# Additions of the staged block sums on VectorE, held in program order

## The chip, the cores and the metric

The kernel runs on one core of one Trainium2 chip. The metric is the device time of one execution in microseconds (us), median of several runs. The core's engines work side by side: PE (TensorE, matrix products), DVE (VectorE), ACT (ScalarE), POOL (GpSimd, here mostly an issuer of transfers) and SP (SyncE, the issuer of the weight transfers). Each engine runs its own instructions strictly in the order in which they stand in its program, and waits where an operand isn't there yet.

## The reference, cut to what matters

One block of a network on 256 tokens of width 2048, all in float32:

```python
h = rms_norm(x, norm_mix_pre)
proj = einsum('bsd,dn->bsn', h, w_in)          # 2048 x 14336 weights, split in 11 parts
y_a = cb * causal_dwconv3(cc * cv, conv_mix_w)
y_b = hgrn2(...)                               # chunked linear recurrence, 8 heads
y_m = softmax(qh @ kh.T / 16) @ vh             # attention over 256 memory rows, 4 heads
merged = (sigmoid(ga) * (y_a @ w_branch[0]) + sigmoid(gb) * (y_b @ w_branch[1])
          + sigmoid(gm) * (y_m @ w_branch[2]))
x = x + rms_norm(merged @ w_out, norm_mix_post)
up_g, up_v = split(rms_norm(x, norm_ffn_pre) @ w_ffn_up)
act = gelu(causal_dwconv3(up_g, conv_ffn_w) + conv_ffn_b) * up_v
x = x + rms_norm(act @ w_ffn_down, norm_ffn_post)
```

The weights are far larger than the on-chip memory and are read once, in the order in which the products need them.

## The kernel before, in words

**Units.** The weight stream is cut into pieces of 1 MB (tile `w`, three buffers) and every piece into two units of 1024 columns. For each unit ACT rounds the weights to `wh` (`halve`, L1107) and DVE forms the remainder `wl = w - wh` (L1108); PE then multiplies by both (L1165 and L1166 where the weights stand still in the array, eight pairs a unit; L1176 to L1178 where the operand does). `wh` and `wl` have four buffers each. The main loop traces `load_to(n + 2)`, `multiply(n)`, `load_to(n + 3)`, then one step of the background queue (norm of x, attention `attend` L298, the recurrence), then one step of the staging. So the `wl` of unit n + 3 is traced ahead of what the staging traces in turn n.

**Stages of the program.** Units 0 to 15 are the lead (memory keys, tile `a_mem`), 16 to 35 the rest of the memory keys and values; 36 to 51 attention queries, with the four attention heads in the background; 52 to 99 three parts of the recurrence's input; 100 to 115 its values; then gates, branches and convolution up to unit 307; `w_out` 308 to 339; then the feed-forward part, whose down projection comes last.

**Staging.** The down projection uses sums of weight blocks for 26 groups (p, j). These sums are made ahead of time in a scratch in DRAM: `load_` (L820) brings 1 MB of `wdown` into a tile `stage` (two buffers) by a DMA that POOL issues (L826), `add_` (L828) makes three additions on DVE in place (one of 1024 columns, L831; two of 512, L834), `store_` (L836) writes the tile to `sums` by another DMA of POOL (L839). A group takes six turns of the main loop: the first traces the store of the group before, the fifth L831, the sixth both L834 and the load of the next group. These turns are units 36 to 115 (thirteen groups) and 250 to 329 (thirteen more), by `STAGE` (L34). The down projection reads the sums back much later.

**Order.** What is traced is not yet the order on an engine: a scheduler lays out each engine's instructions from the dependencies, its own idea of how long things take, and what is ready first. `pin` (L82, `tc.keep_in_program_order`) is an exception: the instruction given to it must stand behind the instruction of its engine that was traced ahead of it. The kernel uses it in the middle and last stages, not in the staging. The scheduler has put the additions of all 26 groups on DVE into the first fifth of the program; those of the second span of turns stand far ahead of the turns that trace them.

Of the kernel before, what the change touches and what calls it, by code (L numbers as in the profile page):

```python
# [13 lines left out]
ALU = mybir.AluOpType  # L14
# [50 lines left out]
def block_kernel(ctx: ExitStack, tc: tile.TileContext, xT, lead, cols, wkvT, wkvN, winT, winN, wbr, wout, wup, wlead, wdown, grow, xN, masks, out):  # L65
    nc = tc.nc
# [15 lines left out]
    pin = tc.keep_in_program_order  # L82
# [734 lines left out]
    def stage(groups):  # L817
        tiles = {}

        def load_(n):  # L820
            if n < len(groups):
                p, j = groups[n]
                tiles[n] = ph.tile([P, 2048], F32, name="stage", tag="stage", bufs=2)
                if n < 2:
                    nc.vector.memset(tiles[n][:, 0:1], 0.0)
                nc.gpsimd.dma_start(tiles[n], wdown[p * DP + j])  # L826

        def add_(n, part):  # L828
            t = tiles[n]
            if part == 0:  # L830
                nc.vector.tensor_tensor(t[:, 0:1024], t[:, 0:1024], t[:, 512:1536], op=ALU.add)  # L831
                return
            for c, low in ((1024, 0), (1536, 1024)):
                nc.vector.tensor_tensor(t[:, c:c + 512], t[:, c:c + 512], t[:, low:low + 512], op=ALU.add)  # L834

        def store_(n):  # L836
            p, j = groups[n]
            stored[p, j] = dram.tile([P, 2048], F32, name=f"sums{p}_{j}")
            nc.gpsimd.dma_start(stored[p, j], tiles.pop(n))  # L839

        load_(0)
        yield
        for n in range(len(groups)):
            for step in range(1, 7):
                if step == 1 and n:
                    store_(n - 1)
                if step == 5:
                    add_(n, 0)
                if step == 6:
                    add_(n, 1)  # L850
                    load_(n + 1)
                yield
        store_(len(groups) - 1)
        yield
# [427 lines left out]
```

## Time and profile before

| | |
|---|---|
| median of 3 runs | 1823.41 us (1821.53 to 1827.84) |
| the profiled execution: time, span | 1823.14 us, 1821.4 us |
| PE busy | 1757.0 us (96%) |
| DVE busy | 1344.9 us (74%) |
| ACT busy | 964.3 us (53%) |
| POOL busy | 36.7 us (2%) |
| moved by DMA | 406.63 MB, 223 GB/s over the span |

The busy share is an average over the whole span. Views that cut the span into stretches (busy time, granted clock and DMA by stretch), the waits by engine and the order of time on one engine say where it is lower. PE's granted clock has two levels, 1.2 and 2.4 GHz, and is given as a share of the higher one. Times of PE are partly modelled, since products overlap in the array, and a few per cent of its records can be missing.

### The profile page before, as it was taken

Reading aid. Unit: us, or ns where it says so; the run is one execution under the profiler, and the core shown is the slowest. Engines: PE = TensorE matmul, PEld = TensorE weight load, DVE = VectorE, ACT = ScalarE, POOL = GpSimd, SP = SyncE. Lnnn points to the kernel's source line nnn. Section 1 sums busy time; section 2 is a strip of 40 time slices with the busy share of each in tenths; the row PEclk is TensorE's granted clock in tenths of the full one; section 3 lists DMA queues with packets and bytes.
Section 4 is the critical chain, followed back from the end, with each engine's and each line's share of the span. In section 5 each row is a group of like instructions: output and inputs, shape, how many; then the busy total and the mean of one; then the engine's idle time right before and its main releaser. Section 6 shows DMA issues by size and latency. Waiting matters only on the chain.

```text
span 1821.4 us, 24557 instructions
## 1 busy us (share of the span) xinstructions
PE 1757.0 (96%) x9336; PEld 1502.6 (82%) x9336; DVE 1344.9 (74%) x2208; ACT 964.3 (53%) x1524; POOL 36.7 (2%) x73
## 2 busy tenths in 40 slices
PE   8998797899999999999999999999999999999998
PEld 7877676688888888888888888888888888888786
DVE  7966675556878888786776568777777777777776
ACT  6733253345565546555665456444444444566565
POOL 0000000000000000000000000000000000000000
PEclk9999898899999999999999999999999999999999
DMA  8798788865454454546555546555555555688895
GB/s 324 290 336 297 275 297 289 304 261 185 162 183 164 167 180 164 183 176 241 185 185 186 190 160 229 186 187 188 187 188 188 187 188 188 204 311 294 301 327 191
DMA packets 62966, 406.63 MB, mean 223 GB/s; under 512 B 7168, under 2 KB 7680, under 8 KB 17024
## 3 DMA queue, kind: packets, MB, share of 16 engines
q1 hardware_dynamic: 53280, 341.73, 52.4%
q0 software_dynamic: 9136, 62.92, 9.6%
q8 instruction: 73, 1.20, 0.3%
q10 hardware_dynamic: 432, 0.41, 0.1%
q14 instruction: 45, 0.37, 0.1%
HBM read 373.58 MB, written 31.46 MB: 222 GB/s over the span
## 4 chain that ended last, share of the span: by engine, by line
PE 80%; issue 9%; DMA 6%; DVE 4%; ACT 1%; POOL 0%; SPq 0%; DVEq 0%; POOLq 0%; ACTq 0%
PE acc L1165 39%; PE acc L1166 20%; DMA stage<-wdown 4%; PE acc L1177 2%; PE acc L1178 2%; PE acc L1176 2%; PE sm L887 2%; PE sm L885 2%; PE sm L886 2%; PE acc L886 2%; PE acc L885 2%; PE acc L887 2%; PE sm L403 1%; DVE wl L1108 1%; DVE stage L834 1%
## 5 line engine op out<-in xcount | busy, mean ns | idle before, releaser
L1165 PE MATMUL acc<-a_x,wh 128*128 128x512 f32 x3072 | 1107.8, 402 | 0.9 <-DVE a_x L100 0.9
L1166 PE MATMUL acc<-a_x,wl 128*128 128x256 f32 x3072 | 874.4, 285 | 19.5 <-DVE wl L1108 19.5
L1107 ACT CAST wh<-w 128x1024 fp32r<-128x1024 f32 (+2 forms) x517 | 537.2, 1040 | 605.0 <-PE acc L1165 358.8
L1108 DVE TENSOR_TENSOR wl<-w,wh 128x1024 fp32r<-128x1024 f32 (+2 forms) x517 | 626.8, 1214 | 273.5 <-ACT wh L1107 272.1
L1165 PEld LDWEIGHTS acc<-a_x,wh 128*128 128x128 f32 x3072 | 584.5, 190 | 141.2 <-DVE a_x L100 1.4
L1166 PEld LDWEIGHTS acc<-a_x,wl 128*128 128x128 f32 x3072 | 588.1, 191 | 21.4 <-DVE wl L1108 21.1
L912 DVE TENSOR_TENSOR wl<-w,wh 128x1024 fp32r<-128x1024 f32 (+1 forms) x110 | 121.5, 1131 | 43.8 <-ACT wh L911 43.5
L911 ACT CAST wh<-w 128x1024 fp32r<-128x1024 f32 (+1 forms) x110 | 105.4, 976 | 63.2 <-PE sm L887 28.5
L118 DVE TENSOR_TENSOR ev<-acc,ev 128x256 f32<-128x256 f32 x245 | 102.5, 418 | 0.5 <-ACT ev L117 0.4
L831 DVE TENSOR_TENSOR stage<-stage 128x1024 f32<-128x1024 f32 x26 | 31.8, 1224 | 79.3 <-DMA stage<-wdown 79.3
L117 ACT COPY ev<-acc 128x256 f32<-128x256 f32 x245 | 88.3, 361 | 1.9 <-PE acc L1166 1.7
L1177 PE MATMUL acc<-wl,a_m 128*128 128x512 f32 x128 | 50.5, 395 | 0.0
L1176 PE MATMUL acc<-wh,a_m 128*128 128x512 f32 x128 | 50.5, 395 | 0.0
L1178 PE MATMUL acc<-wh,a_m 128*128 128x512 f32 x128 | 50.5, 395 | 0.0
L886 PE MATMUL acc<-wl,act 128*128 128x512 f32 x124 | 49.2, 397 | 0.8 <-DVE wl L912 0.8
L887 PE MATMUL sm<-wh,act 128*128 128x512 f32 x124 | 48.9, 395 | 0.0
L887 PE MATMUL acc<-wh,act 128*128 128x512 f32 x124 | 48.9, 395 | 0.0
L886 PE MATMUL sm<-wl,act 128*128 128x512 f32 x124 | 48.9, 395 | 0.0
L885 PE MATMUL sm<-wh,act 128*128 128x512 f32 x124 | 48.9, 394 | 0.0
L885 PE MATMUL acc<-wh,act 128*128 128x512 f32 x124 | 48.6, 396 | 0.1
L1165 PE MATMUL acc<-ya,wh 128*128 128x512 f32 x128 | 46.0, 398 | 0.0
L1165 PE MATMUL acc<-ym,wh 128*128 128x512 f32 x128 | 45.4, 394 | 0.0
(362 smaller groups left out, 2054.4 us busy)
## 6 DMA issues: line engine op xcount, KB each, us to landing
w<-winT SPq DMA_DIRECT2D x104, 1024.0 KB, 4.8
w<-wup SPq DMA_DIRECT2D x84, 1024.0 KB, 4.8
stage<-wdown POOLq DMA_DIRECT2D x26, 1024.0 KB, 7.8
sums<-stage POOLq DMA_DIRECT2D x26, 1024.0 KB, 9.9
w<-wbr SPq DMA_DIRECT2D x24, 1024.0 KB, 4.8
w<-sums SPq DMA_DIRECT2D x20, 1024.0 KB, 6.7
w<-wout SPq DMA_DIRECT2D x16, 1024.0 KB, 4.8
w<-wdown SPq DMA_DIRECT2D x16, 1024.0 KB, 6.8
```

The lines of the kernel that those rows point to most:

```text
L117: nc.scalar.copy(o, ps[:, T:2 * T])
L118: nc.vector.tensor_tensor(o, ps[:, 0:T], o, op=ALU.add)
L885: nc.tensor.matmul(ps, lhsT=hi, rhs=w0_, start=b not in started, stop=False)
L886: nc.tensor.matmul(ps, lhsT=hi, rhs=w1_, start=False, stop=False)
L887: nc.tensor.matmul(ps, lhsT=lo, rhs=w0_, start=False, stop=stop)
L911: nc.scalar.copy(wh[:, 0:n], src)
L912: return wh, wl, lambda: nc.vector.tensor_tensor(wl[:, 0:n], src, wh[:, 0:n], op=ALU.subtract)
L1107: ops = (nc.scalar.copy(wh[:, cs], wsl[:, cs]), nc.vector.tensor_tensor(wl[:, cs], wsl[:, cs], wh[:, cs], op=ALU.subtract))
L1108: nc.vector.tensor_tensor(wl[:, cs], wsl[:, cs], wh[:, cs], op=ALU.subtract))
L1165: hold(nc.tensor.matmul(job.ps, lhsT=wh[:, sl], rhs=a, start=first, stop=False))
L1166: hold(nc.tensor.matmul(job.ps[:, 0:T], lhsT=wl[:, sl], rhs=a[:, 0:T], start=False, stop=last))
L1176: nc.tensor.matmul(job.ps[tt], lhsT=hi, rhs=w0_, start=kt == 0, stop=False)
```

## The change

The four DVE instructions of the staging (two small memsets of the first two tiles and the three additions of each group) are given to `pin`. So each of them must now stand behind the DVE instruction traced ahead of it. Nothing is added or removed; sizes, tiles, transfers and the turns that trace them stay.

```diff
                 if n < 2:
-                    nc.vector.memset(tiles[n][:, 0:1], 0.0)
+                    pin(nc.vector.memset(tiles[n][:, 0:1], 0.0))
                 nc.gpsimd.dma_start(tiles[n], wdown[p * DP + j])
...
             if part == 0:
-                nc.vector.tensor_tensor(t[:, 0:1024], t[:, 0:1024], t[:, 512:1536], op=ALU.add)
+                pin(nc.vector.tensor_tensor(t[:, 0:1024], t[:, 0:1024], t[:, 512:1536], op=ALU.add))
                 return
             for c, low in ((1024, 0), (1536, 1024)):
-                nc.vector.tensor_tensor(t[:, c:c + 512], t[:, c:c + 512], t[:, low:low + 512], op=ALU.add)
+                pin(nc.vector.tensor_tensor(t[:, c:c + 512], t[:, c:c + 512], t[:, low:low + 512], op=ALU.add))
```

**DVE, parts of the recurrence's input (the first span of turns).** Before, from one L831 to the next; L118 and L120 take products out of PE's accumulators (`acc`) into `ev`:

```order
L831 TENSOR_TENSOR stage<-stage 128x1024
L120 TENSOR_TENSOR ev<-ev,rs_x 128x256
L1108 TENSOR_TENSOR wl<-w,wh 128x1024
L834 TENSOR_TENSOR stage<-stage 128x512 x2
L1108 TENSOR_TENSOR wl<-w,wh 128x1024
L118 TENSOR_TENSOR ev<-acc,ev 128x256
L120 TENSOR_TENSOR ev<-ev,rs_x 128x256
L1108 TENSOR_TENSOR wl<-w,wh 128x1024
L831 TENSOR_TENSOR stage<-stage 128x1024
```

The same stretch now; the next L831 follows behind one more L1108:

```order
L831 TENSOR_TENSOR stage<-stage 128x1024
L1108 TENSOR_TENSOR wl<-w,wh 128x1024
L118 TENSOR_TENSOR ev<-acc,ev 128x256
L834 TENSOR_TENSOR stage<-stage 128x512
L120 TENSOR_TENSOR ev<-ev,rs_x 128x256
L834 TENSOR_TENSOR stage<-stage 128x512
L1108 TENSOR_TENSOR wl<-w,wh 128x1024 x2
L118 TENSOR_TENSOR ev<-acc,ev 128x256
L120 TENSOR_TENSOR ev<-ev,rs_x 128x256
L1108 TENSOR_TENSOR wl<-w,wh 128x1024 x2
L118 TENSOR_TENSOR ev<-acc,ev 128x256
L120 TENSOR_TENSOR ev<-ev,rs_x 128x256
```

Three L1108 stood between two L831 before; now six do, one for each unit of a group.

**DVE, third branch (the second span of turns).** L530 and L531 gate and add up the branches, L96 splits the result. Before:

```order
L118 TENSOR_TENSOR ev<-acc,ev 128x256
L530 TENSOR_TENSOR ev<-ev,sg 128x256
L531 TENSOR_TENSOR merged<-merged,ev 128x256
L1108 TENSOR_TENSOR wl<-w,wh 128x1024
L96 TENSOR_TENSOR a_m<-merged,a_m 128x256
L118 TENSOR_TENSOR ev<-acc,ev 128x256
L530 TENSOR_TENSOR ev<-ev,sg 128x256
L531 TENSOR_TENSOR merged<-merged,ev 128x256
L1108 TENSOR_TENSOR wl<-w,wh 128x1024
```

Now:

```order
L118 TENSOR_TENSOR ev<-acc,ev 128x256
L831 TENSOR_TENSOR stage<-stage 128x1024
L530 TENSOR_TENSOR ev<-ev,sg 128x256
L1108 TENSOR_TENSOR wl<-w,wh 128x1024
L531 TENSOR_TENSOR merged<-merged,ev 128x256
L118 TENSOR_TENSOR ev<-acc,ev 128x256
L834 TENSOR_TENSOR stage<-stage 128x512
L530 TENSOR_TENSOR ev<-ev,sg 128x256
L834 TENSOR_TENSOR stage<-stage 128x512
L96 TENSOR_TENSOR a_m<-merged,a_m 128x256
L531 TENSOR_TENSOR merged<-merged,ev 128x256
L1108 TENSOR_TENSOR wl<-w,wh 128x1024
```

The second thirteen groups have moved here, among the work of the third branch and of `w_out`.

**POOL, start of its transfers.** Before, both first loads stand at the program's start:

```order
L826 DMA stage<-wdown 128x2048 x2
L839 DMA sums_1_1227<-stage 128x2048
L826 DMA stage<-wdown 128x2048
L839 DMA sums_3_1434<-stage 128x2048
L839 DMA sums_5_1637<-stage 128x2048
```

Now:

```order
L826 DMA stage<-wdown 128x2048
L839 DMA sums_1_1227<-stage 128x2048
L826 DMA stage<-wdown 128x2048 x2
L839 DMA sums_3_1434<-stage 128x2048
L826 DMA stage<-wdown 128x2048
L839 DMA sums_5_1637<-stage 128x2048
```

The first load waits for its memset, which on DVE now stands behind the `wl` of the memory values instead of at the program's start, and the second load stands behind the first store. SP's program is the same in both; on PE only small products of the norms and of the attention have moved, by a few rows, and only ahead of the recurrence.

## Rows read from the trace of the kernel before

**Rows 1.** Busy time, granted clock (PEclk) and DMA by stretch:
```profile
core 0: us, PE busy (x) PEld busy (x) DVE busy (x) ACT busy (x) POOL busy (x), PEclk, DMA share, GB/s
100.00:370.00 270.00, 220.27 (x1166) 189.74 (x1165) 177.67 (x275) 105.72 (x167) 24.11 (x45) 0.90 0.84 300
260.00:280.00 20.00, 20.00 (x115) 17.37 (x115) 16.63 (x30) 14.19 (x19) 1.61 (x3) 1.00 0.94 349
720.00:740.00 20.00, 20.00 (x116) 17.39 (x115) 18.64 (x39) 14.42 (x31) 0.00 (x0) 1.00 0.45 158
826.00:1050.00 224.00, 224.00 (x1187) 191.39 (x1186) 144.64 (x204) 124.87 (x206) 1.06 (x2) 1.00 0.55 197
1580.00:1800.00 220.00, 219.18 (x943) 176.72 (x943) 164.75 (x184) 137.01 (x161) 5.37 (x10) 1.00 0.85 304
```

**Rows 2.** PE's waits from 100 to 370 us (total, times, longest):
```profile
PE sm L319 <- DVE p L316: 26.3, 6, 9.1
PE acc L1166 <- DVE wl L1108: 19.5, 5, 6.0
PE sm L173 <- DVE rs_x L113: 3.9, 1, 3.9
```

**Rows 3.** The longest of DVE's waits from 100 to 370 us:
```profile
DVE stage L831 <- DMA stage<-wdown: 79.3, 19, 8.7
```

**Rows 4.** Two waits in order of time (start, duration, idle before):
```profile
158.14 1.23 DVE L831 TENSOR_TENSOR stage<-stage 128x1024 f32<-128x1024 f32 x1 [6.53 <-DMA stage<-wdown]
...
160.50 0.66 PE L319 MATMUL sm<-ident,p 128*128 128x128 f32 x2 [7.20 <-DVE p L316]
...
217.49 1.23 DVE L831 TENSOR_TENSOR stage<-stage 128x1024 f32<-128x1024 f32 x1 [4.13 <-DMA stage<-wdown]
...
222.03 0.66 PE L319 MATMUL sm<-ident,p 128*128 128x128 f32 x2 [9.14 <-DVE p L316]
```

**Rows 5.** A load behind its tile's store, and its addition, in order of time:
```profile
322.29 0.53 POOL L826 DMA_DIRECT2D stage<-wdown  x1 [10.02 <-DMA sums<-stage]
...
331.11 1.23 DVE L831 TENSOR_TENSOR stage<-stage 128x1024 f32<-128x1024 f32 x1 [8.66 <-DMA stage<-wdown]
```

**Rows 6.** DMA issues from 100 to 370 us (KB each, median us to landing):
```profile
w<-winT SPq DMA_DIRECT2D x29, 1024.0 KB, 8.3
sums<-stage POOLq DMA_DIRECT2D x23, 1024.0 KB, 10.1
stage<-wdown POOLq DMA_DIRECT2D x22, 1024.0 KB, 7.7
```

**Rows 7.** PE's products from 100 to 370 us by line (count, busy, mean ns):
```profile
L1165 PE MATMUL acc<-a_x,wh 128*128 128x512 f32 x512 | 196.1, 420 | 0.0
L1166 PE MATMUL acc<-a_x,wl 128*128 128x256 f32 x512 | 152.7, 298 | 19.5 <-DVE wl L1108 19.5
...
L308 PE MATMUL sm<-kT,mq 128*128 128x256 f32 x48 | 8.6, 314 | 0.0
...
L331 PE MATMUL sm<-pT,mv 128*128 128x256 f32 x48 | 7.2, 282 | 0.0
```

**Rows 8.** Undisturbed prices: L1165 alone in a later stretch; six attention products:
```profile
1200.00:1260.00 60.00, 60.00 (x171) 31.84 (x171) 1.00 0.55 193
...
204.71 0.88 PE L331 MATMUL sm<-pT,mv 128*128 128x256 f32 x6
```

**Rows 9.** The start of the program, PE and ACT in order of time:
```profile
14.95 1.42 PE L1165 MATMUL acc<-a_mem,wh 128*128 128x512 f32 x3 [2.47 <-ACT wh L1107]
...
13.67 0.51 ACT L99 ACTIVATE a_mem<-w,col_sb 128x256 fp32r<-128x256 f32 x1 [2.96 <-DMA w<-lead]
```

**Rows 10.** DMA issues of the first 20 us, and lead pieces from 20 to 60:
```profile
w<-lead SPq DMA_DIRECT2D x4, 1024.0 KB, 10.3
stage<-wdown POOLq DMA_DIRECT2D x2, 1024.0 KB, 12.8
...
w<-lead SPq DMA_DIRECT2D x3, 1024.0 KB, 4.9
```

## The prediction

> **What bounds the kernel now.** I read the busy time by stretch first. PE is busy all of the time from 826 to 1050 us and all but 0.8 us from 1580 to 1800; from 100 to 370 us it is busy 220.27 of 270 us, and its granted clock is 0.90 there, which between the two levels means a fifth of the stretch at 1.2 GHz [rows 1]. So there is one stretch in which PE loses time. Second, PE's waits in that stretch: 26.3 us before the attention's transposes (L319) for DVE's `p`, 19.5 us before L1166 for DVE's `wl`, 3.9 us for DVE's `rs_x` [rows 2]. All three are waits for DVE. Third, what DVE waits for: 79.3 us in 19 waits, up to 8.7 us, before L831, for the load of `stage` [rows 3]. Fourth, two of them in order of time: DVE stands idle 6.53 us until the load lands at 158.1, adds, only then finishes `p`, and PE, which had stood for 7.20 us, goes on at 160.5; the same with 4.13 us on DVE ahead of PE's longest wait, 9.14 us, at 222 [rows 4]. DVE works in order, so an addition that comes ahead of its data holds up all `wl` and softmax work behind it.
>
> Why the data is late: two buffers serve all groups. The load at 322.29 could be issued only when the store from the same tile had landed, 10.02 us of waiting on POOL, and L831 starts at 331.11 after 8.66 us of waiting on DVE [rows 5]. The landings of this stretch have medians of 10.1 us for a store and 7.7 us for a load [rows 6]. The additions stand closer together on DVE than this ring of two transfers can turn.
>
> **What the lost time is worth.** I count PE's work from 100 to 370 us and price it from undisturbed rows. There are 512 pairs L1165 and L1166 and 96 attention products [rows 7]; 1166 records in all [rows 1], so 46 more. A pair costs 60 / 171 = 0.351 us where nothing disturbs it, an attention product 0.88 / 6 = 0.147 us [rows 8], any other product at most 220 / 943 = 0.233 us, the pace of the last stretch [rows 1]. Sum: 512 x 0.351 + 96 x 0.147 + 46 x 0.233 = 179.7 + 14.1 + 10.7 = 204.5 us. The stretch took 270, so 65.5 us are lost: 49.7 us idle [rows 1], the rest products at the lower clock.
>
> The Trainium skill (Perfetto Trace Analysis, Identifying the Most-Contended Engine) warns that matmul busy time is a poor measure of how near a kernel is to its peak, because products overlap. Taken by busy time alone the loss would be 49.7 us and the forecast below some 16 us higher; the trace agrees with the warning, since products at the lower clock count as busy.
>
> **The change part by part.**
> - The additions of the first thirteen groups keep their span of turns, but six L1108 instead of three stand between two L831. A group now has six units: 6 x 8 x 0.351 = 16.8 us. A tile's ring is store 10.1, load 7.7, two issues of 0.53, and three additions of at most 1.23, together 22.6 us, against two groups or 33.7 us [rows 4 to 6, 8]. The load lands some 11 us before its addition, so the 79.3 us on DVE and with them the 65.5 us on PE go: **-65.5**. What is late next there is PE itself.
> - Not all of PE's waits need be due to the staging. A softmax runs over PE, DVE, ACT, DVE and back while PE has only a few products in between. Of the 26.3 us before L319 the two waits shown, 9.14 and 7.20, stand behind such a load; 10.0 us in the other four remain doubtful, as do 3.9 us for `rs_x` [rows 2, 4]. The second group's load is issued behind the first store, only about four units ahead of its addition, so some 11 us for a landing of 7.7 to 10: at most a wait of a few us, once. Bounds 0 and 30.2 (every wait for `p` and `rs_x` stays); I take half of the doubtful 10.0 and 1 for that load, **+6**, nearer to 0 because the two waits whose cause is seen are the staging's.
> - The start. Two loads of `stage`, 2 MB, leave the first microseconds. They take 12.8 us to land there, beside lead pieces that take 10.3 us, and 4.9 us later on [rows 10]. ACT waits 2.96 us for a piece at 13.67 and PE 2.47 us behind it [rows 9]. Bounds 0 and the difference of the landings, 5.4 us; I take about the wait that is seen, **-3**.
> - The second thirteen groups move to the third branch and `w_out`, 826 to 1050 us, where PE loses nothing now [rows 1]. Each group's additions are at most 3 x 1.23 = 3.7 us of DVE in 16.8 us, 22%, on top of 144.64 / 224 = 65%. DVE is busier than the resulting 87% from 720 to 740 us, 18.64 of 20, and PE loses nothing there [rows 1]. The transfers: 197 GB/s x 224 us = 44.1 MB now, plus 26 of 1.05 MB, 71.4 MB, or 319 GB/s. From 260 to 280 us the queues moved 349 GB/s, staging among it, with PE busy throughout [rows 1]. A weight piece that lands in 8.3 us [rows 6] is still ahead of its turn, since a buffer is refilled two pieces, 4 x 2.8 = 11.2 us, before its `wl` is due, and `wl` runs three units ahead of PE. Cover: the buffers and DVE's idle eighth. Without it each late piece would cost its lateness on PE. Bounds 0 and 14 (the third rival's), I take **+1**.
> - POOL's other transfers: `gp` and `xn` for `w_out` now stand among the second groups' transfers. They wait for tiles that the recurrence and the second branch give back, which is by unit 259, ahead of the additions of the group whose store stands behind them; nothing. `x1`'s copies and the sums' readers come later than the last store; nothing.
>
> Sum against the profiled execution, 1823.1 (the median is 0.3 us higher): 1823.1 - 65.5 + 6 - 3 + 1 = **1761.6, say 1762 us**.
>
> **The rivals.**
> 1. *The softmax sets the pace.* All 26.3 + 3.9 us stay, because DVE's chain is long by itself, and with them their share of the lower clock, 30.2 x 15.8 / 49.7 = 9.6. For it: six waits at eight softmaxes. Against it: the largest stand right behind L831 [rows 2, 4]. It gives 1823.1 - 65.5 - 3 + 30.2 + 9.6 + 1 = 1795.
> 2. *The staging's waits come back, twice.* If a landing grows so that the ring of 22.6 us exceeds 33.7, each L831 again waits, now also in the second span, where nothing was lost. Per group the loss was 65.5 / 23 = 2.85 us (23 stores issued in the stretch [rows 6]); 26 groups give 74: 1823.1 - 65.5 - 3 + 74 = 1829, slower. It decides from 11 us more per turn, landings of 14 us each; the medians are 10.1 and 7.7 [rows 6].
> 3. *Transfers limit the second span.* If the queues give no more than the 300 GB/s of the disturbed stretch [rows 1], 71.4 MB take 238 us instead of 224: +14, so 1762 - 1 + 14 = 1775. For it: a DMA share of 0.55 rises to about 0.9. Against it: 349 GB/s in one slice, and 304 GB/s over 220 us with PE full [rows 1]. The Trainium skill (DMA: Bandwidth & Descriptors, Issuing engines are not separate DMA queues) says that transfers issued by POOL and by SP run on the same 16 DMA engines and interleave, so by that rule the moved staging does take from the weights; the trace agrees, a weight piece landing in 8.3 us beside staging and, as a lead piece, in 4.9 us with little of it [rows 6, 10].
> 4. *The order changes nothing that counts*, 1823: the built order speaks against it, with six L1108 between two L831 and half the groups moved.
>
> **How the numbers follow.** A difference of 0.3%, 5.5 us, is about what a measurement of this kernel can tell from none. Forecast with its own bounds (1750 to 1770): 0.76. Rival 3 with smaller amounts of the same (1770 to 1777): 0.13. Rival 1: 0.07. Rival 2: 0.03. Rival 4: 0.01. The lower end: no residue and the full 5.4 at the start give 1752, and a few missing records in the price of a pair two less, 1750. The range reaches to rival 3, 1777, and leaves out 0.11 and some spill of the others. Faster 0.96, within 0.3% 0.01, slower 0.03.
>
> **What would show it.** Right: no wait of DVE for `stage` beyond one or two of a few us; PE full and its clock at 1.00 from about 100 to 310 us; L831 spread over two spans; PE full in the second span at about 320 GB/s; the lead's wait at 13.67 gone. Wrong: waits before L319 without a `stage` wait ahead of them (rival 1); waits before L831 in both spans (rival 2); ACT waiting for `w` in the second span and PE behind it (rival 3).

## The result and the profile after

The changed kernel takes 1745.37 us (1744.67 to 1745.93), the kernel before 1823.3 us beside it; the ratio is 0.957, with an interval from 0.955 to 0.959. It is faster, as forecast, but by more than forecast: 78.5 us between the two profiled executions (1823.14 and 1744.67 us) where the sum had 61.5, and the median lies 4.6 us under the lower end of the range.

The page of the changed kernel: busy time of each engine, and the shares of the chain that ended last.

```profile
PE 1733.3 (99%) x9336; PEld 1485.4 (85%) x9336; DVE 1340.7 (77%) x2208; ACT 962.3 (55%) x1522; POOL 36.9 (2%) x73
...
PE 97%; DVE 1%; ACT 1%; DMA 1%; issue 0%; ACTq 0%
```

DVE has the same work as before (1344.9 us there). The chain now stays on PE for 97 per cent of the span. Busy time, granted clock and DMA by stretch: the start, the first span of the staging, the second:

```profile
core 0: us, PE busy (x) PEld busy (x) DVE busy (x) ACT busy (x) POOL busy (x), PEclk, DMA share, GB/s
0.00:15.00 15.00, 13.91 (x72) 12.55 (x73) 9.65 (x31) 10.78 (x21) 0.70 (x6) 1.00 0.87 318
97.00:293.00 196.00, 195.94 (x1146) 170.91 (x1145) 147.14 (x235) 102.23 (x164) 11.39 (x21) 1.00 0.75 280
750.00:975.00 225.00, 225.00 (x1199) 192.97 (x1198) 170.30 (x243) 125.65 (x208) 13.91 (x26) 1.00 0.84 310
```

The second row answers to the first of [rows 1]. PE has no gap there and the clock is 1.00 where it was 0.90; 1146 records fit into 196 us where 1166 took 270. The third row is the place of the second thirteen groups: PE is busy throughout although 310 GB/s pass.

What PE waits for in the whole program, by line (total, times, longest), the three largest:

```profile
PE sm L804 <- ACT dg L803: 1.9, 1, 1.9
PE sm L153 <- DVE pad_u L485: 1.1, 1, 1.1
PE acc L1165 <- DVE a_x L100: 0.9, 2, 0.6
```

Nothing of [rows 2] is left. Among DVE's waits there is none for `stage` any more; the largest is now one for ACT, which costs nothing, since PE doesn't wait for `wl`:

```profile
DVE wl L1108 <- ACT wh L1107: 277.4, 298, 2.6
```

The ring on POOL in order of time: each load goes out when the store from its tile has landed, as in [rows 5], but POOL waits for that 4.6 us instead of 10.0, and the additions come so late that nobody waits for the load.

```profile
145.47 0.54 POOL L839 DMA_DIRECT2D sums<-stage  x1 [14.38 <-DVE stage L834]
150.57 0.53 POOL L826 DMA_DIRECT2D stage<-wdown  x1 [4.56 <-DMA sums<-stage]
163.70 0.54 POOL L839 DMA_DIRECT2D sums<-stage  x1 [12.60 <-DVE stage L834]
168.85 0.54 POOL L826 DMA_DIRECT2D stage<-wdown  x1 [4.62 <-DMA sums<-stage]
```

**Where the time went, by landmarks.** Three products stand in the same place of every kernel's program: the first L1165 with `a_x` (unit 36, the attention's queries), the first L1176 with `a_x` (unit 100, the recurrence's values), and the first L562 (behind `w_out`; the feed-forward part is next). Of before, then of after:

```profile
104.16 0.58 PE L1165 MATMUL acc<-a_x,wh 128*128 128x512 f32 x1
...
368.76 0.39 PE L1176 MATMUL acc<-wh,a_x 128*128 128x512 f32 x1
...
1076.03 2.39 PE L562 MATMUL sm<-ones 128*128 128x128 f32 x20
```

```profile
97.31 0.58 PE L1165 MATMUL acc<-a_x,wh 128*128 128x512 f32 x1
...
292.68 0.40 PE L1176 MATMUL acc<-wh,a_x 128*128 128x512 f32 x1
...
997.56 2.39 PE L562 MATMUL sm<-ones 128*128 128x128 f32 x20
```

From such rows each kernel's span falls into four legs. This table, worked out from the profiled executions, carries most of what follows (us):

| kernel | start to a_x | a_x to values | values to L562 | L562 to end |
|---|---|---|---|---|
| before | 104.16 | 264.60 | 707.27 | 745.4 |
| after | 97.31 | 195.37 | 704.88 | 745.3 |
| e1 no additions | 122.56 | 195.44 | 706.79 | 745.6 |
| e2 no staging | 97.60 | 195.54 | 707.09 | 745.7 |
| e3 additions pinned only | 103.96 | 195.51 | 707.10 | 744.8 |
| e4 additions on GpSimd | 137.53 | 223.47 | 706.50 | 745.1 |
| e5 spans side by side | 97.67 | 195.43 | 704.65 | 745.4 |
| e6 more work in place | 97.39 | 204.12 | 705.35 | 746.1 |
| e7 one buffer | 97.89 | 203.80 | 727.36 | 745.4 |
| e8 memsets pinned only | 98.02 | 244.85 | 725.36 | 745.6 |
| e9 one early load | 101.89 | 195.41 | 706.48 | 745.5 |
| e10 after, again | 97.95 | 195.52 | 707.09 | 736.7 |
| e11 as e3, again | 102.94 | 195.55 | 705.03 | 745.4 |
| e12 as e2, again | 97.48 | 195.67 | 704.71 | 745.8 |

From before to after the legs gain 6.85, 69.23, 2.39 and 0.0 us; the last column is worked out from spans that are given to 0.1 us, 745.37 and 745.34 here.

### The profile page after: what moved, and what is told of

It is laid out like the page before. It is cut to its first block, busy times and chain, and to the rows that moved or that the text cites. A ratio compares the mean times of both kernels' runs of the same rounds, so it can differ in the third digit from the quotient of the medians.

```text
span 1742.9 us, 24557 instructions
## 1 busy us (share of the span) xinstructions
PE 1733.3 (99%) x9336; PEld 1485.4 (85%) x9336; DVE 1340.7 (77%) x2208; ACT 962.3 (55%) x1522; POOL 36.9 (2%) x73
## 4 chain that ended last, share of the span: by engine, by line
PE 97%; DVE 1%; ACT 1%; DMA 1%; issue 0%; ACTq 0%
PE acc L1165 47%; PE acc L1166 24%; PE acc L1177 3%; PE acc L1176 3%; PE acc L1178 3%; PE sm L887 2%; PE sm L886 2%; PE sm L885 2%; PE acc L886 2%; PE acc L885 2%; PE acc L887 2%; PE sm L403 1%; PE sm L1165 1%; DMA w<-wdown 1%; PE sm L308 0%; PE sm L1166 0%
## 5 line engine op out<-in xcount | busy, mean ns | idle before, releaser
L1165 PE MATMUL acc<-a_x,wh 128*128 128x512 f32 x3072 | 1091.6, 398 | 0.9 <-DVE a_x L100 0.9
L1166 PE MATMUL acc<-a_x,wl 128*128 128x256 f32 x3072 | 865.1, 282 | 0.0
L1108 DVE TENSOR_TENSOR wl<-w,wh 128x1024 fp32r<-128x1024 f32 (+2 forms) x517 | 627.0, 1213 | 278.6 <-ACT wh L1107 277.4
L1165 PEld LDWEIGHTS acc<-a_x,wh 128*128 128x128 f32 x3072 | 576.9, 188 | 138.5 <-DVE a_x L100 1.5
L1166 PEld LDWEIGHTS acc<-a_x,wl 128*128 128x128 f32 x3072 | 579.0, 188 | 0.3
L118 DVE TENSOR_TENSOR ev<-acc,ev 128x256 f32<-128x256 f32 x245 | 102.3, 418 | 0.8 <-ACT ev L117 0.8
L1176 PE MATMUL acc<-wh,a_m 128*128 128x512 f32 x128 | 50.5, 395 | 0.0
L1165 PE MATMUL acc<-ya,wh 128*128 128x512 f32 x128 | 46.0, 398 | 0.0
L1165 PE MATMUL acc<-ym,wh 128*128 128x512 f32 x128 | 45.4, 394 | 0.0
L1165 PE MATMUL acc<-yb,wh 128*128 128x512 f32 x128 | 45.1, 393 | 0.0
```

Of the source, the lines that this page charges most:

```text
L1108: nc.vector.tensor_tensor(wl[:, cs], wsl[:, cs], wh[:, cs], op=ALU.subtract))
L1165: hold(nc.tensor.matmul(job.ps, lhsT=wh[:, sl], rhs=a, start=first, stop=False))
L1166: hold(nc.tensor.matmul(job.ps[:, 0:T], lhsT=wl[:, sl], rhs=a[:, 0:T], start=False, stop=last))
L1176: nc.tensor.matmul(job.ps[tt], lhsT=hi, rhs=w0_, start=kt == 0, stop=False)
```

## The experiments

The theory: an addition that stands on DVE ahead of its load holds everything behind it on DVE, and through `wl` and `p` PE. The rivals: the 54.5 MB of staging crowd out the weights; the additions' work itself is too much for DVE there; the softmax is slow by itself.

**e1: the kernel before, without its additions.**

```diff
-                nc.vector.tensor_tensor(t[:, 0:1024], t[:, 0:1024], t[:, 512:1536], op=ALU.add)
...
-                nc.vector.tensor_tensor(t[:, c:c + 512], t[:, c:c + 512], t[:, low:low + 512], op=ALU.add)
```

> The kernel before without its three additions a group (L831, L834); the 26 loads into the ring, the 26 stores and every read of the scratch stay, all unpinned as before. Left out of the computation: the sums, the scratch holds the plain blocks. Theory (the additions stand ahead of their loads on DVE and DVE's order holds TensorE): no DVE instruction is left that waits for a load, the stretch 100 to 370 us keeps TensorE full, and what remains of before is the start, where the two early loads cost 6.85 us by the landmarks of the two traces: 1745.4 + 6.9 = 1752 us, 1748 to 1757. Rival A (congestion: the transfers of 26 groups packed into the first stretch delay the weights, and thinning them is what gained): the same transfers run there at least as densely, so 1805 to 1823 us. Rival B (the softmax chain of L319 and L173 sets the pace and the sums only add to it): half of the loss stays, about 1785 us.

Measured: 1772.57 us, ratio 0.971 (0.969 to 0.974), 20 us over the theory's number, 12 under rival B's and 32 under rival A's, so the total alone decides nothing. The windows tell why (lines of code move up by three here, L1165 is L1162):

```profile
15.00:122.00 107.00, 95.78 (x429) 78.80 (x430) 73.18 (x115) 59.80 (x98) 11.78 (x22) 0.91 1.01 417
122.00:318.00 196.00, 195.95 (x1145) 170.87 (x1144) 125.95 (x205) 102.34 (x163) 14.61 (x27) 1.00 0.85 329
...
122.00:230.00 108.00, 107.95 (x647) 94.45 (x646) 71.22 (x127) 54.80 (x95) 12.37 (x23) 1.00 1.00 396
```

From 122 to 318 us, the stretch in dispute, PE is full and the leg takes 195.44 us, as in the changed kernel, although the 26 groups' transfers are packed more densely than ever: the last load goes out at 234 us, in the kernel before at 357, and from 122 to 230 us, with the ring still turning, DMA moved 396 GB/s. So the transfers did not cost the 69 us. What the theory had missed is the first row: with no addition in its way the ring turns from the first microsecond on, the queues move 417 GB/s, and PE starves for the first weights, which have no work ahead of them: 25.3 us in that leg, where the loads of before cost 6.9. ACT's largest wait up to 122 us is for the lead; in the kernel before it waits 8.0 us for it, in the changed kernel 0.9:

```profile
ACT a_mem L99 <- DMA w<-lead: 18.7, 8, 3.4
```

**e2: the changed kernel without staging.** `STAGE` (L34) is empty, and the scratch's reads go to `wdown`.

```diff
-STAGE = (range(36, 116), range(250, 330))
+STAGE = ()
...
-            nc.sync.dma_start(hold["sums"], stored[p, j])
+            nc.sync.dma_start(hold["sums"], src)
```

> The changed kernel without its staging: no loads into the ring, no additions, no stores; where the scratch was read, the same number of bytes is read from wdown. Left out of the computation: the sums. This is the floor for any order of the additions. Theory: the pinned staging is wholly covered by TensorE's work, so 1744 to 1746 us, the 0.6 us or so that TensorE waits for wl and a_x in the changed kernel aside. Rival A (the 26 groups' 54.5 MB still delay the weights): 1730 to 1740 us. Rival C (the pace of the projections' pairs, 0.348 us in one stretch and 0.353 in another, comes from DVE's or the rings' accesses to SBUF): pairs at 0.348 in all stretches, about 1736 us.

Measured: 1747.49 us, ratio 0.958 (0.956 to 0.960), the changed kernel's within the interval, though 1.5 us over the theory's range. The second leg is the changed kernel's too, 195.54; the third is 2.2 us longer, 707.09, on which e10 to e12 bear. The pinned staging costs nothing that can be measured; rivals A and C fall.

**e3: only the additions pinned.**

```diff
-                    pin(nc.vector.memset(tiles[n][:, 0:1], 0.0))
+                    nc.vector.memset(tiles[n][:, 0:1], 0.0)
```

> The changed kernel with the two memsets of L825 not pinned: the additions stand where the change puts them, and the first two loads go out at the start again, as in the kernel before. Theory: the only difference left is the start, where the two loads travel beside the first weights; the landmarks say 6.1 us by the first L1176 and 6.85 us by the first L1165 of the recurrence, so 1745.4 + 6.1 to 6.9 = 1751.5 to 1752.3 us, range 1749 to 1754; the first L99 on ACT waits for lead until about 13.7 us instead of 9.0 us. Rival D (the early start came from the additions that stood on DVE in the load phase, 18.6 to 90 us, and not from the loads): 1744 to 1747 us.

Measured: 1752.88 us, ratio 0.961 (0.958 to 0.963), 5.4 us over e2 on the same chip, with 103.96 us to the first L1165 instead of 97.60. So the two early loads cost the start, not the additions that stood there; rival D falls. The start is the memsets' part of the change, the rest the additions'.

**e4: the additions on GpSimd, nothing pinned.**

```diff
-                nc.vector.tensor_tensor(t[:, 0:1024], t[:, 0:1024], t[:, 512:1536], op=ALU.add)
+                nc.gpsimd.tensor_tensor(t[:, 0:1024], t[:, 0:1024], t[:, 512:1536], op=ALU.add)
...
-                nc.vector.tensor_tensor(t[:, c:c + 512], t[:, c:c + 512], t[:, low:low + 512], op=ALU.add)
+                nc.gpsimd.tensor_tensor(t[:, c:c + 512], t[:, c:c + 512], t[:, low:low + 512], op=ALU.add)
```

> The kernel before with the three additions a group on GpSimd instead of DVE, nothing pinned; all work is there and the 26 groups are staged in the first stretch as fast as the ring goes. Theory: GpSimd issues the loads and the stores and now waits for the loads itself, DVE and TensorE don't, so only the start is lost: 1752 us, 1748 to 1760, with no wait of DVE for stage. Rival A (congestion): the transfers are as dense as before, 1800 to 1823 us. Rival E (GpSimd's additions slow DVE's own two-input additions while they run; the trace of before has no such row): 26 groups of 2.6 us on DVE, bounded by DVE standing still as long as GpSimd adds, at twice DVE's time 26 x 5.2 = 135 us of the first stretch, where DVE has 23 per cent idle: up to 60 us over 1752.

Measured: 1814.39 us, ratio 0.994 (0.993 to 0.996). No DVE instruction waits for `stage`, yet nearly the whole gain is gone: 40.2 us in the first leg against the changed kernel, 28.1 in the second. Rival E's mechanism is there. Its highest number, 1812 us, is passed by 2; of the first leg's 40.2 us e1 lost 25.3 without any addition, so how much of them is GpSimd's and how much the transfers' isn't settled. DVE's lines from a_x to values, first e4, then the same leg of e2 (busy, mean ns, idle before):

```profile
L1108 DVE TENSOR_TENSOR wl<-w,wh 128x1024 fp32r<-128x1024 f32 x65 | 103.5, 1597 | 38.5 <-ACT wh L1107 38.5
L120 DVE TENSOR_TENSOR ev<-ev,rs_x 128x256 f32<-128x256 f32 x23 | 16.4, 715 | 0.6
L118 DVE TENSOR_TENSOR ev<-acc,ev 128x256 f32<-128x256 f32 x31 | 12.8, 414 | 0.0
...
L316 DVE TENSOR_SCALAR p<-p,mx 128x256 f32<-128x256 f32 x8 | 4.8, 599 | 0.3
```

```profile
L1108 DVE TENSOR_TENSOR wl<-w,wh 128x1024 fp32r<-128x1024 f32 x64 | 78.2, 1223 | 53.9 <-ACT wh L1107 53.7
L118 DVE TENSOR_TENSOR ev<-acc,ev 128x256 f32<-128x256 f32 x31 | 12.9, 418 | 0.0
L120 DVE TENSOR_TENSOR ev<-ev,rs_x 128x256 f32<-128x256 f32 x23 | 9.7, 423 | 0.6
...
L316 DVE TENSOR_SCALAR p<-p,mx 128x256 f32<-128x256 f32 x8 | 2.8, 353 | 0.3
```

L1108 and L120, which read two tiles, are 1.3 and 1.7 times as long; L118, which reads one operand from the accumulators, is not. It isn't only the two-tile operations: L316, one tile and a column of scalars, is 1.7 times as long. In order of time:

```profile
159.95 2.42 POOL L831 TENSOR_TENSOR stage<-stage 128x1024 f32<-128x1024 f32 x1 [3.21 <-DMA stage<-wdown]
...
160.15 3.31 DVE L1108 TENSOR_TENSOR wl<-w,wh 128x1024 fp32r<-128x1024 f32 x1 [1.26 <-ACT wh L1107]
163.37 0.41 DVE L118 TENSOR_TENSOR ev<-acc,ev 128x256 f32<-128x256 f32 x1
```

L1108 starts 0.20 us behind GpSimd's addition and ends 1.1 us after that ends, so it stood until GpSimd was done. The Trainium skill (SBUF — State Buffer, SBUF: two separate sides) says that DVE and GpSimd share one pair of ports, which whoever starts first holds for its whole instruction, a two-tile DVE operation among those that need it; these rows agree. So e4 swaps one hold of DVE for another and says nothing of transfers.

**e5: all 26 groups again in one stretch, pinned.**

```diff
-STAGE = (range(36, 116), range(250, 330))
+STAGE = (range(36, 116), range(116, 196))
```

> The changed kernel with its second span of groups at units 116 to 195 instead of 250 to 329: all 26 groups, loads, additions and stores, follow one another between about 77 and 520 us, each addition still behind the DVE instruction traced ahead of it. Theory (it is the place of the additions in DVE's order that cost the time, not how many groups there are or how near they stand): no wait of DVE for stage, first a_x L1165 to first hv L1176 stays at 195.4 us, the whole at 1745 to 1750 us. Rival B2 (half of the gain came from thirteen groups leaving the busy first stretch, so that DVE or the transfers are crowded when they come back beside it): a loss of up to half of 69 us, 1760 to 1785 us, with waits of TensorE for wl or p between 290 and 520 us.

Measured: 1744.76 us, ratio 0.958 (0.956 to 0.960). The first thirteen groups pass in a second leg of 195.43 us, and PE is full while the others follow them, at 294 GB/s and with DVE at 186 of 227 us:

```profile
293.00:520.00 227.00, 227.00 (x1238) 196.05 (x1237) 186.16 (x324) 127.36 (x207) 13.34 (x25) 1.00 0.79 294
```

DVE waits for `stage` twice in the whole run, 6.5 us together, and no wait of PE comes of it. So rival B2 falls: thirteen groups beside the others cost nothing. The pace isn't that of before, though: one group in 17.6 us (L831 from 121.0 to 560.1 us) against one in 11.4. At the pace of before and above it e1 has the transfers without loss; all of the additions' work at that pace, with none of them ahead of its load, is in no run.

**e6: more work beside the additions, in their place.**

```diff
                 pin(nc.vector.tensor_tensor(t[:, 0:1024], t[:, 0:1024], t[:, 512:1536], op=ALU.add))
+                pin(nc.vector.tensor_scalar(t[:, 0:1024], t[:, 0:1024], 1.0, None, op0=ALU.mult))
...
                 pin(nc.vector.tensor_tensor(t[:, c:c + 512], t[:, c:c + 512], t[:, low:low + 512], op=ALU.add))
+                pin(nc.vector.tensor_scalar(t[:, c:c + 512], t[:, c:c + 512], 1.0, None, op0=ALU.mult))
```

> The changed kernel with each addition followed, in its place, by a multiplication by one over the same columns: 2.6 us more of DVE a group, 13 groups in each span, so DVE is busy 147 + 34 = 181 of 196 us in the first span and 170 + 34 = 204 of 225 us in the second. Theory (place, not work): the three units by which wl runs ahead cover it, 1745 to 1749 us. Rival F (DVE's work is what costs, and the gain came from spreading it): TensorE waits for wl and p in both spans, 1755 to 1813 us (the upper end with all of 26 x 2.6 us on the path).

Measured: 1753.98 us, ratio 0.963 (0.961 to 0.965), 5 us over the theory's range and at rival F's edge. The multiplications are shorter than the additions, 0.69 and 0.42 us, so a group has 0.69 + 2 x 0.42 = 1.5 us more, not 2.6, and a span 20 us. Of 26 groups one cost something:

```profile
143.09 1.22 DVE L831 TENSOR_TENSOR stage<-stage 128x1024 f32<-128x1024 f32 x1 [6.64 <-DMA stage<-wdown]
...
150.16 0.69 PE L319 MATMUL sm<-ident,p 128*128 128x128 f32 x2 [6.09 <-DVE p L316]
```

The second group's load goes out behind the first group's store; the longer additions delay that store, so the load goes out at 128.79 us instead of 125.63, and it lands 14.3 us later instead of 8.3. In the changed kernel it had landed 1.2 us ahead of its L831 (at 135.09); here L831 waits 6.64 us for it, and PE 6.09 us for a `p` behind it, in a stretch of lowered clock (0.90 from 130 to 165 us, PE busy 28.9 of 35 us). That is 8.7 us in the second leg; the second span loses nothing although DVE has 20 us more to do there. So far the work is covered; an addition ahead of its load is not. This pair of rows is the whole theory in one event: 6.6 us on DVE, 8.7 on PE. (Lines from L832 on move down by up to two here, L1165 is L1167.)

**e7: one buffer for the staging.**

```diff
-                tiles[n] = ph.tile([P, 2048], F32, name="stage", tag="stage", bufs=2)
+                tiles[n] = ph.tile([P, 2048], F32, name="stage", tag="stage", bufs=1)
```

> The changed kernel with one buffer for the staging instead of two, so that each load waits for the store of the group ahead. By the legs of the changed kernel one turn takes 5.1 + 5.7 + 3.5 + 1.1 = 15.4 us in the first span, under the 15 to 20 us from group to group, and 9.6 + 8.1 + 3.7 + 1.1 = 22.5 us in the second, over the 17.3 us there. Theory: nothing lost before 293 us; in the second span DVE waits for stage again, and TensorE loses what the lead of wl (three units, 3 x 2.8 us) doesn't cover: 12 x 5.2 - 8.4 = 54 us at the landing times of the changed kernel, less as far as they shorten with fewer transfers under way (at the 6.6 and 5.9 us of its whole run, a turn of 17.1 us, nothing): 1745 to 1799 us, 1765 in the middle. Rival G (a pinned addition costs nothing wherever its load comes, since wl stands ahead): 1745 us in any case, in spite of waits of DVE for stage.

Measured: 1776.59 us, ratio 0.976 (0.974 to 0.978). DVE's waits for `stage` from 97 to 302 us (up to the first L1176), from 302 to 370 us (the last groups of the first span), and from 700 to 1010 us:

```profile
DVE stage L831 <- DMA stage<-wdown: 31.4, 6, 8.0
```

```profile
DVE stage L831 <- DMA stage<-wdown: 23.6, 3, 10.1
```

```profile
DVE stage L831 <- DMA stage<-wdown: 52.4, 12, 9.0
```

The first span loses 8.4 us in the second leg and 7.0 in the third: from the first L1176 to the first product of L403, behind that span, it takes 74.35 us, in the changed kernel 67.36. So it loses 15.4 of DVE's 55.0 us, and the second span, from there to the first L562, 13.3 to 15.5 of 52.4 (653.0 us against 637.5 in the changed kernel and 639.7 in e2). Rival G falls: with the same work, pinned in the same way, the loss is back as soon as the loads are late, so pinning is worth something only as long as the ring keeps ahead. The total is inside the theory's range, but its "nothing in the first span" is wrong: from L831 to the store it isn't 3.5 us, since the three additions stand apart on DVE; in the changed kernel it is 145.47 - 135.09 = 10.4 us for the second group, whose L831 is this:

```profile
135.09 1.22 DVE L831 TENSOR_TENSOR stage<-stage 128x1024 f32<-128x1024 f32 x1
```

**e8: the kernel before with only the memsets pinned.**

```diff
-                    nc.vector.memset(tiles[n][:, 0:1], 0.0)
+                    pin(nc.vector.memset(tiles[n][:, 0:1], 0.0))
```

> The kernel before with the two memsets of L825 alone pinned, so that the ring's first load goes out at about 77 us instead of 1.5 us and the additions stand again one behind the other on DVE, 26 groups ahead of their loads. Theory (from the first group on the ring's pace holds DVE): first addition at about 86 us, 25 more at the 11.4 us of the kernel before (19 groups from 145.4 to 362.8 us), so the last L831 at about 371 us, 8 us later than in the kernel before, of which some 7 come back because it stands eleven rows further down DVE's order: 1815 to 1832 us, 1824 in the middle; the start gains its 6.9 us and gives it back. Rival H (each group costs a fixed 2.5 us wherever the ring begins): only the start's gain stays, 1816 us, with the last L831 at about 356 us.

Measured: 1812.14 us, ratio 0.995 (0.994 to 0.997): under the theory's range, and 4 us under rival H. The last L831 starts later than either said:

```profile
386.56 1.23 DVE L831 TENSOR_TENSOR stage<-stage 128x1024 f32<-128x1024 f32 x1 [6.08 <-DMA stage<-wdown]
```

That is 24 us later than before (362.8), and still nothing more was lost: 49.5 us in the second leg and some 18 in the third, together 68 where before has 69. What I had sized wrongly is the place. Counted along DVE's instructions without the staging's, in the trace of e2, the last addition of before stands at about 284 us and that of e8 at 308 to 314 us. So the ring ends 24 us later and the place that it holds stands 25 to 30 us further down: the loss is the ring's end less the place, 363 - 284 = 79 (with the start's 6) and 387 - 311 = 76 us on DVE, of which PE lost 76 and 68 by the first product of L403, against e2. The start's 6 us are gained; the total fell by 10. That a group costs a fixed amount (H) isn't excluded by this run.

**e9 to e12, side by side on one chip**: the changed kernel with one early load (only the second memset pinned), the changed kernel (e10), e3 (e11) and e2 (e12) again.

```diff
-                    pin(nc.vector.memset(tiles[n][:, 0:1], 0.0))
+                    (pin if n else lambda i: i)(nc.vector.memset(tiles[n][:, 0:1], 0.0))
```

> The changed kernel with only the first memset of L825 not pinned: one of the two first loads goes out at the start, the other where the change puts it. Nothing else differs, and the order on TensorE, ACT and SP is that of the changed kernel. With both early the first L1165 of the recurrence came 6.65 us later (103.96 against 97.31 us). Theory (a load at the start costs the time in which its 1.05 MB pass at the 318 GB/s of the first 15 us, 3.3 us each): first a_x L1165 at 100.6 us, the whole 3.3 us over the changed kernel run beside it. Rival (only a transfer that goes out beside the first weights with another one costs, or only the second one does): 0 to 1 us, or 5.5 to 7 us.

> The changed kernel once more, beside its relatives on one chip. Theory: 1744 to 1746 us, and at least as fast as the kernel without staging. On the 2.3 us between hv's first L1176 and the first L562 that it took less than the kernel before (704.9 against 707.3 us): if that is of the program, 704.9 again here; if it is of the single execution or the chip, 704.7 to 707.3 at random.

> The changed kernel with both memsets not pinned, once more, beside the changed kernel on one chip: two loads at the start. Theory: 6.65 us over it by the first a_x L1165; and if the pace between hv's first L1176 and the first L562 is of the program, 707.1 us there again, so 8 to 9 us over it as a whole.

> The kernel without staging once more (the sums are left out; the scratch's reads are reads of wdown), beside the changed kernel on one chip. Theory: the same time as the changed kernel within 3 us; if the pace between hv's first L1176 and the first L562 is of the program, 707.1 us there again, 2.2 us over the changed kernel, so that the changed kernel is the faster of the two by that, in spite of its 54.5 MB more.

Measured: 1748.23, 1745.62, 1749.31 and 1745.83 us, ratios 0.960 (0.958 to 0.962), 0.958 (0.955 to 0.960), 0.961 (0.959 to 0.963) and 0.959 (0.957 to 0.960). The changed kernel and the one without staging are equal. e11 is 3.7 us over the changed kernel, where 8 to 9 were expected. One early load delays the first L1165 by 3.9 us against e10, two by 5.0 here and by 6.4 in e3 against e2. In the table's first column the eight kernels without an early load stand at 97.31 to 98.02 us, the one with a single early load at 101.89, and the three with two and nothing else early (before, e3, e11) at 102.94 to 104.16. So the second load costs less than the first, 1.0 to 2.3 us after 3.9 to 4.6, as far as one execution with a single load can tell; the theory's 3.3 us each isn't borne out. ACT's wait for the `lead` piece in e11 is that of [rows 9]; in the changed kernel the piece is used from 9.01 us on:

```profile
14.70 0.51 ACT L99 ACTIVATE a_mem<-w,col_sb 128x256 fp32r<-128x256 f32 x1 [2.97 <-DMA w<-lead]
```

```profile
9.01 0.51 ACT L99 ACTIVATE a_mem<-w,col_sb 128x256 fp32r<-128x256 f32 x1 [0.46 <-DMA w<-lead]
```

The third leg answers its question too: 704.88 and 707.09 us for the changed kernel, 707.10 and 705.03 for e3, 707.09 and 704.71 for e2. The 2.4 us belong to the execution, not to the program, and so not to the change.

## Why the prediction was right and wrong

- **The bound and its cause: right.** e1 takes the additions away and keeps the transfers, e5 keeps both in another order and at a slower pace, and in both the leg falls from 264.6 to 195.4 us. That an addition's wait costs and not its work is seen in DVE's idle time of before [rows 3] and in e6 and e7, where the loss comes back with the waits; the one thing not run is named at e5. The ring's arithmetic, one turn inside two groups' time, held, but for the second group, whose load landed only 1.2 us ahead of its addition.
- **The sum.** It missed the two profiled executions' difference by 17.0 us: 6.0 in the residue, 3.9 at the start, 3.7 in the worth of the first stretch, 1 in the second span, and 2.4 that belong to the execution.
- **The term -65.5: too small by 3.7.** The leg lost 69.2 us. PE's work in the stretch was priced at 204.5 us; the same products, from start to start in the trace of the changed kernel, take 201.2. The price of the attention products was wrong: 0.147 us was the length of six overlapping products, 0.88, by six. What such a group adds to the chain is 0.71, or 0.118 each, as the chain of after shows. By their starts the 96 products take 11.7 us, not 14.1; the 46 others, priced at an upper bound, 7.5, not 10.7; and the 512 pairs 181.9, not 179.7, which hides part of the two errors.

```profile
125.73 0.71 PE sm L331 x6
```

- **The residue +6: wrong, it is 0.** All of the waits for `p` and `rs_x` were the staging's, the "doubtful" four too; with no addition ahead of its load not one of any size is left, and e2 shows the same leg. The step that failed was to halve the four waits for want of a row that ties them to an L831, instead of following each of them back. The trace of before had the rows: each of the six waits before L319 stands 2.4 to 7.2 us behind an L831 that waited 2.05 to 7.28 us for its load. The longest of the doubtful four:

```profile
231.10 1.22 DVE L831 TENSOR_TENSOR stage<-stage 128x1024 f32<-128x1024 f32 x1 [7.28 <-DMA stage<-wdown]
...
235.56 0.69 PE L319 MATMUL sm<-ident,p 128*128 128x128 f32 x2 [4.13 <-DVE p L316]
```

  The one late second load that I allowed for is there in e6, not in the changed kernel.
- **The start -3: too small.** 6.85 us between the two executions, 5 to 6.4 by e3 and e11. The step that failed was to take one wait of ACT for a late piece of the lead, 2.96 us at 13.67, as the term: ACT had waited 3.34 us for the piece before it as well, where the changed kernel waits 0.48.

```profile
8.75 0.51 ACT L99 ACTIVATE a_mem<-w,col_sb 128x256 fp32r<-128x256 f32 x1 [3.34 <-DMA w<-lead]
```

```profile
6.28 0.51 ACT L99 ACTIVATE a_mem<-w,col_sb 128x256 fp32r<-128x256 f32 x1 [0.48 <-DMA w<-lead]
```

  From 10 to 20 us PE then stood idle for 2.5 us, and its granted clock was 0.83, a third of the time at the lower level; the changed kernel, PE busy throughout, has 1.00. Before and after:

```profile
10.00:20.00 10.00, 7.50 (x32) 6.07 (x33) 6.31 (x12) 5.90 (x13) 0.00 (x0) 0.83 0.95 383
```

```profile
10.00:20.00 10.00, 10.00 (x59) 8.78 (x58) 9.77 (x17) 10.00 (x19) 0.00 (x0) 1.00 0.99 347
```

  The 2.1 MB of the two loads at the 351 GB/s of the first 15 us of before, 6.0 us, would have been the better estimate of the sum, though e9 shows that the two loads don't share it evenly. e1 shows a term of the same kind at its largest, 25.3 us.
- **The second span +1: right in kind, it is 0.** Its cover was real: 310 GB/s with PE full. The 2.4 us by which it came out shorter are the execution's.
- **The rivals.** The softmax (1) and the waits that come back (2) did not occur; e7 shows that the second was a real mechanism, with one buffer instead of two. Transfers as a limit (3) did not occur at 310 GB/s here or at 396 in e1.
- **The range.** Its lower end left out the residue and took the start at its bound, 1752; the start, the price of PE's work and the pace of the execution together, 1.5 + 3.7 + 2.4 us, went beyond that. The last of the three is chance.

## What to carry to other kernels

An instruction that stands on an in-order engine ahead of its transfer holds up everything behind it, however small its own work; put it where the engine's own pace brings its turn later than the transfer's landing, and its work is free as far as the engine has idle time there. To size such a loss, take the time at which the last held instruction runs and subtract the time at which its place in the order would come without the hold (79 and 76 us here, for 76 and 68 lost). At the start of this program, where nothing runs ahead of the weights, other transfers cost time: one load of 1 MB about 4 us, two 5 to 7, a ring that turns freely 25; later the same transfers were free.

## What was not expected of the hardware

- GpSimd's two-tile additions stop DVE: the mean of L1108 goes from 1223 to 1597 ns, of L120 from 423 to 715, and of L316, with one tile and a column, from 353 to 599, while L118, with one operand in the accumulators, stays at 414 (e4).
- The queues gave 417 GB/s over 107 us, loads and stores mixed (e1), where before I had seen 349 in one slice [rows 1].
- The same program runs its products at two paces. In e10 the feed-forward part's L1165 and L1166 come every 0.347 us, in after every 0.353, at a granted clock of 1.00 in both, and the one execution is 8.6 us shorter from L562 on. The third leg's 2.4 us are the same thing: from 760 to 900 us the pairs come every 0.348 us in after, e11 and e12, every 0.352 in e10, e2 and e3. The mean length of L1165 from 1100 to 1700 us, of after, then of e10:

```profile
L1165 PE MATMUL acc<-a_x,wh 128*128 128x512 f32 x1141 | 403.2, 397 | 0.0
```

```profile
L1165 PE MATMUL acc<-a_x,wh 128*128 128x512 f32 x1145 | 397.0, 392 | 0.0
```

What decides between the two paces stays open; no run was made on it. A single profiled execution's total therefore can't tell differences of some 2 to 9 us of this kernel. The first leg alone repeats better: the eight executions without early loads lie within 0.7 us.
